# A decoder trunk on one core: decays from mid-chunk, corner products for four heads at once, and a joined first load

## The chip, the core and the metric

The kernel runs on one core of a Trainium2 chip. The metric is the device time of one execution in microseconds (us). The engines are named as the profile names them: PE is the matrix engine (PEld its weight loads), DVE the vector engine, ACT the scalar engine, POOL the GpSimd engine, SP the engine that issues most DMAs.

## The reference, cut to what matters

One decoder layer on 256 tokens, with 16 learned tokens put ahead (272 in all), width 2048, everything in float32:

```python
proj = rmsnorm(h) @ w_in
o_fox = forgetting_attention(fq, fk, fv, ff, b_forget)      # 8 heads of 128, causal softmax with decay
g_log = log_sigmoid(ga @ w_alpha2 + b_alpha) / 16
o_gla = gated_linear_attention(gq, gk, gv, g_log)           # 4 heads, keys 256, values 512 wide, chunks of 64
o_gla = head_rmsnorm(o_gla, gla_norm_g) * silu(gr)
y = sigmoid(gate_fox) * (o_fox @ w_o_fox) + sigmoid(gate_gla) * (o_gla @ w_o_gla)
h = h + y @ w_out
h = h + squared_relu(rmsnorm(h) @ w1) @ w2
out = rmsnorm(h)[:, 16:]
```

In the linear attention the logarithms of the decays are summed inside each chunk of 64 tokens (b). A query is multiplied by exp(b), a key by exp(-b), and a key that is seen from a later chunk also by the decays of the whole chunks between. The 272 tokens make four chunks of 64 and a fifth of 16.

## The kernel before

Activations lie with channels on the partitions and tokens along the free dimension. Every weight block of 128 output channels is streamed once from HBM in two halves (`raw`), cut into a high part by ACT (`whi`, line 120) and a remainder by DVE (`wlo`, line 121), both in the type fp32r; activations are cut into two parts likewise (`x`). A block is then either `gemm2` (lines 136 and 137: 512 columns with the high part, 256 with the remainder, for 16 slices) or, where all 272 tokens are wanted, `gemm_all` (lines 153 to 155: three products of 272 columns). Small products inside the attention (scores, transposes, parts of the outputs) are in plain float32, and such a product of line 518, 688, 739 or 740 stands as two records in the trace.

The order around the products is written by hand and then adjusted by a scheduler that simulates the program. `later(n, fn)` runs `fn` after n more blocks; so the attention's small products are put between the blocks of the streamed weights, in one queue of PE that is worked off in order. PSUM has three banks for blocks (`pg`) and five for everything else (`px`).

- Opening (lines 291 to 348): SP issues the first tile of `h`, two of seven weight blocks, the second tile of `h`, two more blocks, then three. `warm` is five products of ones that PE runs in the meantime (line 298). In stage 0 ACT makes `x` (line 311) and cuts the weights (line 266), DVE the remainders (lines 312 and 267).
- `decays(hd)` (line 386) makes, for a pair of key tiles of one GLA head, the running sums `za` (line 403), exp of them for queries (`eb_all`) and keys (`en_all`), and `ends`, the decay of each whole chunk (line 408).
- `gla_head(hd)` (line 468): `kx` holds per pair of chunks the keys, the keys carried into the next chunk and the next chunk's keys; `kd` the same carried one chunk further; `qd` the decayed queries, `rq` those of the later chunks carried back. `scores` (line 512) makes seven products, each over two key tiles: 48, 64, 64, 144, 64, 16 and 16 columns. The third to sixth have 128 columns of keys, the others 64. `turn` transposes the values; `vg` gathers the last 16 tokens of the head's four value tiles.
- `fox_head(hd)` (line 665): `scores`, `turn_v`, `turn_p` (lines 714 to 734) and `out_v` (line 736). The 272 tokens are 128 + 128 + 16 for keys and 16 + 128 + 128 for blocks of queries, so each head has two corners of 16 x 16 in its probabilities: transposes of 16 columns (lines 718, 729, 730), a product `vb` by `pT` with 144 columns and a product of the corner with 16 (line 740).

Of the kernel before, what the change touches and what calls it, by code (L numbers as in the profile page):

```python
# [7 lines left out]
F32 = mybir.dt.float32  # L8
# [57 lines left out]
def trunk(ctx: ExitStack, tc: tile.TileContext, hT, w_small, w_all, consts, w_alpha2, out):  # L66
# [222 lines left out]


    load_a, load_b = load_stage(0, 0), load_stage(0, 1)
    load_h(nc.sync, 0, 1)
    load_a(0, 2)
    load_h(nc.sync, 1, 1)
    load_a(2, 2)
    load_b(0, 3)
    for cols in (NT, NT, NT, NT, P):
        nc.tensor.matmul(warm[:, 0:cols], ones[:, 0:P], ones[:, 0:cols], start=True, stop=True)
    for s in range(1, 3):
        load_h(nc.sync, 2 * s, 2)  # L300
# [2 lines left out]
    for s in range(KT // 2):  # L303
# [5 lines left out]
        for kk in range(2):  # L309
            k = 2 * s + kk  # L310
            nc.scalar.activation(x[:, k, 0, :], h[:, k, 0:NA], AF.Identity, scale=gain(0, k))
# [68 lines left out]
    both = take(NA)  # L380
    fc = take(NA)[32:40]
    eb_all = lin.tile([P, 8, NT], F32, name="eb_all")
    ends = lin.tile([P, 8, 4], F32, name="ends")
    en_all = lin.tile([P, 8, NA], F32, name="en_all")

    def decays(hd):
# [21 lines left out]
        nc.vector.tensor_copy(ends[:, two, :], eb_all[:, two, C - NM - 1 : NT : C])  # L408
# [45 lines left out]
    NB = NA - 4 * C  # L454
    at0 = padded(lin, "at0", NT)
    at1 = padded(lin, "at1", NT - Q1)
    vz = padded(lin, "vz", P)
    az = padded(lin, "az", 4 * NB)
    v0 = [lin.tile([P, GLA_DV], F32R, name=n) for n in ("v0h", "v0l")]

# [7 lines left out]
    def gla_head(hd, sg, ready=None):  # L468
# [6 lines left out]
        qd = ready[0] if ready else att.tile([P, 2, NT], F32, tag="qd", name=nm("qd"))  # L475

        def keys(i, ps):
            def four(ap):
# [12 lines left out]
            for i in range(2):  # L491
                keys(i, gemm_all(next_weights(), x))
        for i in range(2):
            t = qd[:, i, :] if ready else total(gemm2(next_weights(), x[:, :, :, NM:NA]))
            nc.vector.scalar_tensor_tensor(qd[:, i, :], t, GLA_DK ** -0.5, eb[:, i, :], op0=ALU.mult, op1=ALU.mult)
        nc.vector.tensor_tensor(kx[:, :, :, C : 2 * C], kx[:, :, :, 0:C],
                                end[:, :, 0:4:2].unsqueeze(3).to_broadcast([P, 2, 2, C]), op=ALU.mult)

        kd = att.tile([P, 2, 2, 2 * C], F32, tag="kd", name=nm("kd"))
        nc.vector.tensor_tensor(kd, kx[:, :, :, C : 3 * C],  # L500
                                end[:, :, 1:4:2].unsqueeze(3).to_broadcast([P, 2, 2, 2 * C]), op=ALU.mult)

        rq = att.tile([P, 2, NT - Q1], F32, tag="rq", name=nm("rq"))
        nc.gpsimd.tensor_copy(rq[:, :, 0 : 2 * C], qd[:, :, Q1 : Q1 + 2 * C])
        nc.vector.tensor_tensor(rq[:, :, 2 * C :], qd[:, :, Q1 + 2 * C :], end[:, :, 3:4].to_broadcast([P, 2, NB]),
                                op=ALU.mult)
        nc.vector.tensor_tensor(rq[:, :, C:], rq[:, :, C:], end[:, :, 2:3].to_broadcast([P, 2, C + NB]), op=ALU.mult)

# [3 lines left out]
        def scores():  # L512
            pa = bank(px, "pa")
            p0, p1, pz = pa[:, 0:NT], pa[:, NT : 2 * NT - Q1], pa[0:C, 2 * NT - Q1 : 2 * NT - Q1 + NB]

            def score(dst, k, q):
                for a in range(2):
                    nc.tensor.matmul(dst, k[:, a], q[:, a, :], start=(a == 0), stop=(a == 1))  # L518

            Q0 = Q1 - C  # L520
# [19 lines left out]


        v1 = att.tile([P, GLA_DV], F32, tag="v1", name=nm("v1"))
        vg = att.tile([P, 4 * NB], F32, tag="vg", name=nm("vg"))
        pv = []

        def turn(i, vT):
# [3 lines left out]
            nc.tensor.transpose(pv[0][:, cols], vT[:, 0:P], ident)  # L550
            nc.tensor.transpose(pv[1][:, cols], vT[:, P : 2 * P], ident)
            if i == 3:
                p2 = bank(px, "p2")[0 : 4 * NB, 0:P]
# [3 lines left out]
                nc.scalar.copy(vz[0 : 4 * NB, :], p2)  # L557

        for i in range(4):
            ps = gemm_all(next_weights(), x)  # L560
# [57 lines left out]
    qd0 = att.tile([P, 2, NT], F32, tag="qd", name=nm("qd"))  # L618
    for i in range(2):
        total(first_ps[4 + i], qd0[:, i, :])  # L620
    ps = bank(pg, "psa")[:, 0:NA]
# [40 lines left out]
    vcs = [padded(late, f"vc{i}", P) for i in range(2)]  # L662
    pcs = [padded(late, f"pc{i}", NM) for i in range(2)]

    def fox_head(hd):
        fk = att.tile([P, NA], F32, tag="fk", name=nm("fk"))
# [41 lines left out]
        vc, pc = vcs[hd % 2], pcs[hd % 2]  # L708


        pT = att.tile([P, NM + P], F32, tag="pT", name=nm("pT"))
        nc.gpsimd.memset(pT[:, 0:NM], 0.0)

        def turn_v():
            pv = bank(px, "pv")
            nc.tensor.transpose(pv[:, 0:P], vT[:, 0:P], ident)
            nc.tensor.transpose(pv[:, P : 2 * P], vT[:, P : 2 * P], ident)
            nc.tensor.transpose(pv[0:NM, 2 * P : 3 * P], vT[:, 2 * P :], ident)
            va.extend(split(att, "va", pv[:, 0:P]))
            nc.scalar.copy(vb, pv[:, P : 2 * P])  # L720
            nc.scalar.copy(vc[0:NM, :], pv[0:NM, 2 * P : 3 * P])

        def turn_p():
            pt, pu = bank(px, "pt"), bank(px, "pu")
# [3 lines left out]
            nc.tensor.transpose(pt[:, 2 * P : 3 * P], pr_[:, q1 : q1 + P], ident)  # L728
            nc.tensor.transpose(pu[0:NM, 0:P], pr_[:, P : P + NM], ident)
            nc.tensor.transpose(pu[0:NM, P : 2 * P], pr_[:, q1 + 2 * P : q1 + NA], ident)  # L730
            nc.scalar.copy(pT[:, NM:], pt[:, 0:P])
            pa.extend(split(att, "pa", pt[:, P : 3 * P], 1))
            nc.vector.tensor_copy(pT[0:NM, 0:NM], pu[0:NM, P - NM : P])
            nc.vector.tensor_copy(pc[0:NM, :], pu[0:NM, 2 * P - NM : 2 * P])

        def out_v():
            po = bank(px, "pof")
            three(po[:, 0:NT], va, pa, True, False)
            nc.tensor.matmul(po[:, P - NM : NT], vb, pT, start=False, stop=False)
            nc.tensor.matmul(po[:, NT - NM : NT], vc, pc, start=False, stop=True)  # L740
# [256 lines left out]
```

## Time and profile before

| | before |
|---|---|
| median of 3 runs | 1609.93 us (1609.76 to 1610.15) |
| the profiled execution | 1609.59 us, its span 1607.9 us |
| granted clock of PE, mean | 0.998 |
| DVE busy | 1053.7 us (66%) |
| ACT busy | 787.4 us (49%) |
| POOL busy | 101.9 us (6%) |

The span runs from the first to the last instruction of the core; the execution's time is 1.7 us longer. A row of the timeline has the start in us from the beginning of the span, the us that the row covers, engine, line, operation, out<-in, the stationary and the moving operand, and xN, the number of records merged in it; what stands in brackets is the idle time before it and what ended it. PE records overlap, since their ends are modelled: what a product costs is read from the distance of its start to the start of the next. A group has the number of records, busy time, mean ns of one, and the idle time before them.

### The profile page before, as it was taken

Reading aid. Unit: us, or ns where it says so; the run is one execution under the profiler, and the core shown is the slowest. Engines: PE = TensorE matmul, PEld = TensorE weight load, DVE = VectorE, ACT = ScalarE, POOL = GpSimd, SP = SyncE. Lnnn points to the kernel's source line nnn. Section 1 sums busy time; section 2 is a strip of 40 time slices with the busy share of each in tenths; the row PEclk is TensorE's granted clock in tenths of the full one; section 3 lists DMA queues with packets and bytes.
Section 4 is the critical chain, followed back from the end, with each engine's and each line's share of the span. In section 5 each row is a group of like instructions: output and inputs, shape, how many; then the busy total and the mean of one; then the engine's idle time right before and its main releaser. Section 6 shows DMA issues by size and latency. Waiting matters only on the chain.

```text
span 1607.9 us, 25392 instructions
## 1 busy us (share of the span) xinstructions
PE 1597.0 (99%) x9878; PEld 1436.1 (89%) x9878; DVE 1053.7 (66%) x1603; ACT 787.4 (49%) x1221; POOL 101.9 (6%) x158
## 2 busy tenths in 40 slices
PE   9999999999999999999999999999999999999997
PEld 8999999999998888888888888888888888888887
DVE  7887757576655555555677776567655776567655
ACT  7655444454445444444555544444444444444563
POOL 1011000110000000000011000000000000000022
PEclk9999999999999999999999999999999999999999
DMA  9454545554555566556566555665565555656552
GB/s 322 156 160 146 182 154 177 184 171 158 158 158 180 187 187 190 187 187 190 174 203 188 186 190 188 188 189 187 187 193 186 189 188 189 191 186 190 185 183 97
DMA packets 86745, 293.09 MB, mean 182 GB/s; under 512 B 9128, under 2 KB 17072, under 8 KB 86496
## 3 DMA queue, kind: packets, MB, share of 16 engines
q1 hardware_dynamic: 86016, 289.62, 56.9%
q8 instruction: 77, 1.26, 0.3%
q0 software_dynamic: 176, 1.12, 0.2%
q10 hardware_dynamic: 432, 0.72, 0.1%
q14 instruction: 44, 0.36, 0.1%
HBM read 289.32 MB, written 2.11 MB: 181 GB/s over the span
## 4 chain that ended last, share of the span: by engine, by line
PE 99%; DMA 0%; issue 0%; POOL 0%; SPq 0%; ACT 0%; POOLq 0%; DVE 0%; ACTq 0%
PE ps L136 51%; PE ps L137 26%; PE psa L155 5%; PE psa L154 5%; PE psa L153 5%; PE ps L328 1%; PE pa L518 1%; PE ps L866 1%; PE ps L333 1%; PE ps L850 0%; DMA raw<-w_all_dram 0%; PE po L584 0%; POOL o L914 0%; PE pq L688 0%; PE p L550 0%
## 5 line engine op out<-in xcount | busy, mean ns | idle before, releaser
L121 DVE TENSOR_TENSOR wlo<-raw,whi 128x1024 fp32r<-128x1024 f32 x522 | 640.8, 1228 | 462.6 <-ACT whi L120 461.8
L120 ACT CAST whi<-raw 128x1024 fp32r<-128x1024 f32 x522 | 548.0, 1050 | 732.6 <-PE ps L136 502.9
L136 PE MATMUL ps<-x,whi 128*128 128x512 f32 x1952 | 685.9, 394 | 0.0
L137 PE MATMUL ps<-x,wlo 128*128 128x256 f32 x1952 | 547.8, 281 | 0.0
L136 PEld LDWEIGHTS ps<-x,whi 128*128 128x128 f32 x1952 | 366.4, 188 | 83.2
L137 PEld LDWEIGHTS ps<-x,wlo 128*128 128x128 f32 x1952 | 367.4, 188 | 0.2
L136 PE MATMUL ps<-a,whi 128*128 128x512 f32 x960 | 335.8, 395 | 0.0
L137 PE MATMUL ps<-a,wlo 128*128 128x256 f32 x960 | 269.9, 282 | 0.0
L136 PEld LDWEIGHTS ps<-a,whi 128*128 128x128 f32 x960 | 180.1, 188 | 40.8
L137 PEld LDWEIGHTS ps<-a,wlo 128*128 128x128 f32 x960 | 181.7, 189 | 0.3
L155 PE MATMUL psa<-x,whi 128*128 128x272 f32 x624 | 181.3, 291 | 0.0
L153 PE MATMUL psa<-x,whi 128*128 128x272 f32 x624 | 181.3, 290 | 0.0
L154 PE MATMUL psa<-x,wlo 128*128 128x272 f32 x624 | 179.7, 288 | 0.0
L153 PEld LDWEIGHTS psa<-x,whi 128*128 128x128 f32 x624 | 118.2, 189 | 0.5
L154 PEld LDWEIGHTS psa<-x,wlo 128*128 128x128 f32 x624 | 117.5, 188 | 0.0
L155 PEld LDWEIGHTS psa<-x,whi 128*128 128x128 f32 x624 | 117.2, 188 | 0.1
L136 PE MATMUL ps<-og,whi 128*128 128x512 f32 x256 | 89.9, 393 | 0.0
L136 PE MATMUL ps<-y,whi 128*128 128x512 f32 x256 | 89.1, 392 | 0.0
L792 POOL TENSOR_TENSOR acc<-acc,hsq 128x256 f32<-128x256 f32 x26 | 28.4, 1092 | 771.4 <-ACT hsq L791 771.4
L137 PE MATMUL ps<-y,wlo 128*128 128x256 f32 x256 | 71.8, 281 | 0.0
L137 PE MATMUL ps<-og,wlo 128*128 128x256 f32 x256 | 71.8, 280 | 0.0
L165 DVE TENSOR_TENSOR evt<-ps,evb 128x256 f32<-128x256 f32 x158 | 65.8, 417 | 0.2 <-ACT evb L162 0.2
(294 smaller groups left out, 1413.4 us busy)
## 6 DMA issues: line engine op xcount, KB each, us to landing
raw<-w_all_dram SPq DMA_DIRECT2D x537, 512.0 KB, 3.9
raw<-w_all_dram SPq DMA_DIRECT2D x8, 384.0 KB, 6.6
h<-hT_dram SPq DMA_DIRECT2D x7, 275.0 KB, 7.0
negc<-fdram POOLq DMA_DIRECT2D x1, 1088.0 KB, 6.3
out_dram<-o SPq DMA_DIRECT2D x2, 512.0 KB, 2.7
raw<-w_all_dram SPq DMA_DIRECT2D x2, 256.0 KB, 3.6
out_dram<-o ACTq DMA_DIRECT2D x2, 256.0 KB, 3.0
room<-w_small_dram SPq DMA_DIRECT2D x1, 320.0 KB, 7.7
```

The source lines that it names most:

```text
L120: nc.scalar.copy(hi[:, k, :], r)
L121: nc.vector.tensor_tensor(lo[:, k, :], r, hi[:, k, :].bitcast(F32), op=ALU.subtract)
L136: nc.tensor.matmul(ps, hi, x, start=first, stop=False)
L137: nc.tensor.matmul(ps[:, 0:NT], lo, x[:, 0, :], start=False, stop=last)
L153: nc.tensor.matmul(ps[:, 0:n], hi, x[:, k, 0, :], start=(k == 0), stop=False)
L154: nc.tensor.matmul(ps[:, 0:n], lo, x[:, k, 0, :], start=False, stop=False)
L155: nc.tensor.matmul(ps[:, 0:n], hi, x[:, k, 1, :], start=False, stop=(k == KT - 1))
L165: nc.vector.tensor_tensor(t, ps[:, 0:NT], b, op=ALU.add)
L328: nc.tensor.matmul(ps, hi, x[:, k, :, NM:NA], start=st, stop=False)
L333: nc.tensor.matmul(ps[:, 0:NT], lo, x[:, k, 0, NM:NA], start=False, stop=sp)
L518: nc.tensor.matmul(dst, k[:, a], q[:, a, :], start=(a == 0), stop=(a == 1))
L792: nc.gpsimd.tensor_tensor(acc, acc, sq, op=ALU.add)
```

## The change

1. In `decays` the running sums are counted from the middle of each chunk: half of a chunk's last sum is taken off all its sums before the exponentials. `ends` then holds five factors for carrying a query or key across chunks, made by a small exponential.
2. In GLA's scores the queries lie in one tile `qx` with the carried copies beside the own ones. Two products, of 208 and 80 columns, replace the four with 128 columns of keys (64, 144, 64 and 16). `kd` and `rq` are gone; keys are carried once. The product of the last 16 tokens moves ahead of the two.
3. In FoX the corners of four heads are gathered by POOL (`vg`, `pgr`), transposed together and multiplied in one product, masked by `same`, and added to the output after every fourth head (`out_corners`, `fill_corners`). The per-head corner transposes and the corner product go, and `pT` has 128 columns instead of 144.
4. In the opening `h`'s first two tiles are one load, `warm` has four products, and the first two weight blocks are cut slice by slice.
5. In GLA the padded tile of the last 16 tokens is the transpose's input (`vg`, 128 columns) instead of its output.

```diff
-    load_h(nc.sync, 0, 1)
+    load_h(nc.sync, 0, 2)
     load_a(0, 2)
-    load_h(nc.sync, 1, 1)
     load_a(2, 2)
     load_b(0, 3)
-    for cols in (NT, NT, NT, NT, P):
+    for cols in (NT, NT, NT, NT):
         nc.tensor.matmul(warm[:, 0:cols], ones[:, 0:P], ones[:, 0:cols], start=True, stop=True)
...
             if s == 0:
-                wa[3](2 * kk, 2)
+                wa[3](0, 2, slice(kk, kk + 1))
...
         if s == 0:
+            wa[3](2, 2)
...
+        e, half = ends[:, two, :], tmp.tile([P, 2, 4], F32, tag="half", name=nm("half"))
+        nc.vector.tensor_scalar(half, za[:, :, C - 1 : 4 * C : C], 0.5, None, op0=ALU.mult)
+        nc.vector.tensor_tensor(e[:, :, 1:4], half[:, :, 0:3], half[:, :, 1:4], op=ALU.add)
+        nc.vector.tensor_tensor(e[:, :, 4:5], e[:, :, 2:3], e[:, :, 3:4], op=ALU.add)
+        nc.vector.tensor_copy(e[:, :, 0:1], half[:, :, 3:4])
+        nc.scalar.activation(e, e, AF.Exp, scale=1.0 / 16.0)
+        four = za[:, :, 0 : 4 * C].rearrange("p a (c s) -> p a c s", s=C)
+        nc.vector.tensor_tensor(four, four, half.unsqueeze(3).to_broadcast([P, 2, 4, C]), op=ALU.subtract)
...
-        nc.vector.tensor_copy(ends[:, two, :], eb_all[:, two, C - NM - 1 : NT : C])
...
-            nc.vector.scalar_tensor_tensor(qd[:, i, :], t, GLA_DK ** -0.5, eb[:, i, :], op0=ALU.mult, op1=ALU.mult)
+            for q, n, at in ((0, Q1, 0), (Q1, Q3, NT)):
+                nc.vector.scalar_tensor_tensor(qx[:, i, at : at + n], t[:, q : q + n], GLA_DK ** -0.5,
+                                               eb[:, i, q : q + n], op0=ALU.mult, op1=ALU.mult)
...
-        nc.vector.tensor_tensor(kd, kx[:, :, :, C : 3 * C],
-                                end[:, :, 1:4:2].unsqueeze(3).to_broadcast([P, 2, 2, 2 * C]), op=ALU.mult)
...
-        nc.gpsimd.tensor_copy(rq[:, :, 0 : 2 * C], qd[:, :, Q1 : Q1 + 2 * C])
...
+        def seen(dst, src, c):
+            nc.vector.tensor_tensor(dst, src, end[:, :, c : c + 1].to_broadcast(list(dst.shape)), op=ALU.mult)
...
+        q2, q3, qz = (qx[:, :, NT + c : NT + d] for c, d in ((0, C), (C, Q3), (Q3, Q3 + NB)))
+        nc.gpsimd.tensor_copy(qz, q3[:, :, C:])
+        seen(q3[:, :, C:], q3[:, :, C:], 0)
+        seen(qx[:, :, Q1 : Q1 + C], q2, 2)
+        seen(qx[:, :, Q1 + C : NT], q3, 4)
...
-            score(p0[0:C, 0:Q0], kx[:, :, 0, 0:C], qd[:, :, 0:Q0])
-            score(p1[0:C, 0:C], kx[:, :, 1, 0:C], qd[:, :, Q1 : Q1 + C])
-            score(p0[:, Q0:Q1], kx[:, :, 0, C:], qd[:, :, Q0:Q1])
-            score(p0[:, Q1:], kd[:, :, 0, :], rq)
-            score(p1[:, C : 2 * C], kx[:, :, 1, C:], qd[:, :, Q1 + C : Q1 + 2 * C])
-            score(p1[:, 2 * C :], kd[:, :, 1, :], qd[:, :, Q1 + 2 * C :])
-            score(pz, kz.rearrange("p a b t -> p a (b t)"), qd[:, :, Q1 + 2 * C :])
+            score(p0[0:C, 0:Q0], kx[:, :, 0, 0:C], qx[:, :, 0:Q0])
+            score(p1[0:C, 0:C], kx[:, :, 1, 0:C], q2)
+            score(pz, kz.rearrange("p a b t -> p a (b t)"), qz)
+            score(p0[:, Q0:], kx[:, :, 0, C:], qx[:, :, Q0:NT])
+            score(p1[:, C:], kx[:, :, 1, C:], q3)
...
+    def corners(t):
+        return t.rearrange("p (c q) -> p c q", q=P)[:, :, P - NM :]
...
+        for c in range(2):
+            nc.gpsimd.tensor_copy(vg[:, four, c, :], vT[:, P * (1 + c) : P * (1 + c) + NM])
...
-            nc.tensor.transpose(pv[0:NM, 2 * P : 3 * P], vT[:, 2 * P :], ident)
...
-            nc.scalar.copy(vc[0:NM, :], pv[0:NM, 2 * P : 3 * P])
...
+            for c, at0 in ((0, P), (1, q1 + 2 * P)):
+                nc.gpsimd.tensor_copy(pgr[:, four, c, :], pr_[:, at0 : at0 + NM])
...
-            nc.tensor.transpose(pu[0:NM, 0:P], pr_[:, P : P + NM], ident)
-            nc.tensor.transpose(pu[0:NM, P : 2 * P], pr_[:, q1 + 2 * P : q1 + NA], ident)
...
-            nc.tensor.matmul(po[:, P - NM : NT], vb, pT, start=False, stop=False)
-            nc.tensor.matmul(po[:, NT - NM : NT], vc, pc, start=False, stop=True)
+            nc.tensor.matmul(po[:, P:NT], vb, pT, start=False, stop=True)
...
+            nc.scalar.copy(og4[:, four], corners(po[:, 0:NT]))
+
+        def out_corners():
+            pu = bank(px, "pu")
+            vz, pz = (t.rearrange("p h c t -> p (h c t)") for t in (vg, pgr))
+            nc.tensor.transpose(pu[:, 0:P], vz, ident)
+            nc.tensor.transpose(pu[:, P : 2 * P], pz, ident)
+            nc.scalar.copy(vz, pu[:, 0:P])
+            nc.vector.tensor_tensor(pz.rearrange("p (b q) -> p b q", q=NM), same,
+                                    pu[:, 2 * P - NM : 2 * P].unsqueeze(1).to_broadcast([P, NC, NM]), op=ALU.mult)
+            later(1, lambda: fill_corners(pu, vz, pz))
+
+        def fill_corners(pu, vz, pz):
+            nc.tensor.matmul(pu[:, 2 * P : 3 * P], vz, pz, start=True, stop=True)
+            nc.vector.tensor_tensor(og4, og4, pu[:, 2 * P : 3 * P].rearrange("p (h c q) -> p h c q", c=2, q=NM),
+                                    op=ALU.add)
+            hi, lo = (of[:, hd - 3 : hd + 1, o, :].rearrange("p h (c q) -> p h c q", q=P)[:, :, :, P - NM :]
+                      for o in range(2))
+            split_to(hi, lo, og4)
...
+        if four == 3:
+            later(3, out_corners)
```

As the changed program is laid out on PE, `out_corners`' transposes follow the `vb` product of head 3, and stand between `out_v`'s first and second product for head 7. The corner product follows one block later. After head 7 the first eight k-slices of the output projection's two FoX blocks run four and four: the part that reads heads 0 to 3 comes ahead of 19 products of the next block, the part that reads heads 4 to 7 behind them. In GLA's first head the first score products stand 28 products into the fourth value block (3 before).

More of the change, by code (lines that the diff above doesn't have):

```diff
@@ L382, in trunk @@
     eb_all = lin.tile([P, 8, NT], F32, name="eb_all")
-    ends = lin.tile([P, 8, 4], F32, name="ends")
+    ends = lin.tile([P, 8, 5], F32, name="ends")
     en_all = lin.tile([P, 8, NA], F32, name="en_all")
@@ L456, in trunk @@
     at1 = padded(lin, "at1", NT - Q1)
-    vz = padded(lin, "vz", P)
+    vg = padded(lin, "vg", P)
     az = padded(lin, "az", 4 * NB)
@@ L474, in gla_head @@
         kz = att.tile([P, 2, 4, NB], F32, tag="kz", name=nm("kz"))
-        qd = ready[0] if ready else att.tile([P, 2, NT], F32, tag="qd", name=nm("qd"))
+        qx = att.tile([P, 2, 2 * NT - 6 * NB], F32, tag="qx", name=nm("qx"))
+        Q0, Q3 = Q1 - C, NT - Q1
         def keys(i, ps):
@@ L493, in gla_head @@
         for i in range(2):
-            t = qd[:, i, :] if ready else total(gemm2(next_weights(), x[:, :, :, NM:NA]))
-            nc.vector.scalar_tensor_tensor(qd[:, i, :], t, GLA_DK ** -0.5, eb[:, i, :], op0=ALU.mult, op1=ALU.mult)
-        nc.vector.tensor_tensor(kx[:, :, :, C : 2 * C], kx[:, :, :, 0:C],
-                                end[:, :, 0:4:2].unsqueeze(3).to_broadcast([P, 2, 2, C]), op=ALU.mult)
-        kd = att.tile([P, 2, 2, 2 * C], F32, tag="kd", name=nm("kd"))
-        nc.vector.tensor_tensor(kd, kx[:, :, :, C : 3 * C],
-                                end[:, :, 1:4:2].unsqueeze(3).to_broadcast([P, 2, 2, 2 * C]), op=ALU.mult)
-        rq = att.tile([P, 2, NT - Q1], F32, tag="rq", name=nm("rq"))
-        nc.gpsimd.tensor_copy(rq[:, :, 0 : 2 * C], qd[:, :, Q1 : Q1 + 2 * C])
-        nc.vector.tensor_tensor(rq[:, :, 2 * C :], qd[:, :, Q1 + 2 * C :], end[:, :, 3:4].to_broadcast([P, 2, NB]),
-                                op=ALU.mult)
-        nc.vector.tensor_tensor(rq[:, :, C:], rq[:, :, C:], end[:, :, 2:3].to_broadcast([P, 2, C + NB]), op=ALU.mult)
+            t = ready[0][:, i, :] if ready else total(gemm2(next_weights(), x[:, :, :, NM:NA]))
+            for q, n, at in ((0, Q1, 0), (Q1, Q3, NT)):
[3 more added lines that the diff above has]
+            nc.vector.tensor_tensor(dst, src, end[:, :, c : c + 1].to_broadcast(list(dst.shape)), op=ALU.mult)
+        nc.vector.tensor_tensor(kx[:, :, :, C : 2 * C], kx[:, :, :, 0:C],
+                                end[:, :, 1:4:2].unsqueeze(3).to_broadcast([P, 2, 2, C]), op=ALU.mult)
+        q2, q3, qz = (qx[:, :, NT + c : NT + d] for c, d in ((0, C), (C, Q3), (Q3, Q3 + NB)))
[3 more added lines that the diff above has]
+        seen(qx[:, :, Q1 + C : NT], q3, 4)
         def scores():
@@ L542, in gla_head @@
         v1 = att.tile([P, GLA_DV], F32, tag="v1", name=nm("v1"))
-        vg = att.tile([P, 4 * NB], F32, tag="vg", name=nm("vg"))
+        vz = att.tile([P, P], F32, tag="vz", name=nm("vz"))
         pv = []
@@ L552, in turn @@
             if i == 3:
-                p2 = bank(px, "p2")[0 : 4 * NB, 0:P]
+                p2 = bank(px, "p2")[:, 0:P]
                 nc.tensor.transpose(p2, vg, ident)
@@ L556, in turn @@
                 nc.scalar.copy(v1, pv[1])
-                nc.scalar.copy(vz[0 : 4 * NB, :], p2)
+                nc.scalar.copy(vz, p2)
         for i in range(4):
@@ L617, in trunk @@
     ts = [total(ps) for ps in first_ps[0:4]]
-    qd0 = att.tile([P, 2, NT], F32, tag="qd", name=nm("qd"))
+    qd0 = att.tile([P, 4, NT], F32, tag="so", name=nm("qd"))[:, 0:2, :]
     for i in range(2):
@@ L661, in trunk @@
     BL = ((0, NM + P, 0), (1, NA, NM + P))
-    vcs = [padded(late, f"vc{i}", P) for i in range(2)]
-    pcs = [padded(late, f"pc{i}", NM) for i in range(2)]
+    NC = P // NM
+    same = scan[:, 0:P].rearrange("p (b q) -> p b q", q=NM)
+    nc.gpsimd.memset(same, 1.0)
+    for sign, base in ((-1, 0), (1, NM - 1)):
+        nc.gpsimd.affine_select(same, same, pattern=[[sign * NM, NC], [0, NM]], compare_op=ALU.is_ge, fill=0.0,
+                                base=base, channel_multiplier=-sign)
+    corner = {}
+    def corners(t):
+        return t.rearrange("p (c q) -> p c q", q=P)[:, :, P - NM :]
     def fox_head(hd):
@@ L707, in fox_head @@
         vb = att.tile([P, P], F32, tag="vb", name=nm("vb"))
-        vc, pc = vcs[hd % 2], pcs[hd % 2]
-        pT = att.tile([P, NM + P], F32, tag="pT", name=nm("pT"))
-        nc.gpsimd.memset(pT[:, 0:NM], 0.0)
+        pT = att.tile([P, P], F32, tag="pT", name=nm("pT"))
+        four = hd % 4
+        if four == 0:
+            corner["v"], corner["p"], corner["o"] = (att.tile([P, 4, 2, NM], F32, tag=t, name=nm(t), bufs=1)
+                                                     for t in ("vg", "pgr", "og4"))
+        vg, pgr, og4 = corner["v"], corner["p"], corner["o"]
+        for c in range(2):
+            nc.gpsimd.tensor_copy(vg[:, four, c, :], vT[:, P * (1 + c) : P * (1 + c) + NM])
         def turn_v():
@@ L728, in turn_p @@
             nc.tensor.transpose(pt[:, 2 * P : 3 * P], pr_[:, q1 : q1 + P], ident)
[L729 to L731 removed]
+            nc.scalar.copy(pT, pt[:, 0:P])
             pa.extend(split(att, "pa", pt[:, P : 3 * P], 1))
[L733 to L734 removed]
         def out_v():
```

3 lines of the change are left out of this document (1 added, 2 removed).

## The prediction

> **What bounds the kernel now.** I read the page first, then PE's waits, then the timeline of PE around the small products and of the first 12 us.
>
> ```profile
> span 1607.9 us, 25392 instructions
> PE 1597.0 (99%) x9878; PEld 1436.1 (89%) x9878; DVE 1053.7 (66%) x1603; ACT 787.4 (49%) x1221; POOL 101.9 (6%) x158
> ```
>
> PE is busy for 1597.0 of 1607.9 us. As ends of products are modelled, that alone proves nothing; what does is the view of PE's waits, which holds three waits in all, each one time:
>
> ```profile
> PE warm L298 <- DVE ones L189: 1.3, 1, 1.3
> PE ps L328 <- ACT whi L266: 1.0, 1, 1.0
> PE pn L890 <- ACT sq L871: 0.7, 1, 0.7
> ```
>
> Two lie in the opening, one in the tail. In between PE never stops for weights, a bank or an operand. So each record that leaves PE's queue there takes its whole spacing off the time, work moved to DVE, ACT and POOL costs nothing unless it makes PE stop, and outside that stretch only the opening is changed.
>
> **GLA's scores.** First the scores of the last head, then the end of a FoX output; start, us covered, engine, line, operands, records. The first row merges eight records of 64 key columns and the four of the second row, which a window that begins later shows alone.
>
> ```profile
> 283.72 1.27 PE L518 MATMUL pa<-qd,kx 128*64 128x48 f32 x12
> 284.33 0.66 PE L518 MATMUL pa<-qd,kx 128*128 128x64 f32 x4
> 284.82 0.71 PE L518 MATMUL pa<-rq,kd 128*128 128x144 f32 x4
> 285.37 0.56 PE L518 MATMUL pa<-qd,kx 128*128 128x64 f32 x4
> 285.76 0.57 PE L518 MATMUL pa<-qd,kd 128*128 128x16 f32 x4
> 286.26 0.40 PE L518 MATMUL pa<-qd,kz 128*64 128x16 f32 x4
> 286.60 0.33 PE L550 MATMUL p<-cons,vT 128*128 128x128 f32 x1
> ...
> 395.74 0.41 PE L739 MATMUL pof<-pT,vb 128*128 128x144 f32 x2
> 395.99 0.29 PE L740 MATMUL pof<-pc,vc 128*128 128x16 f32 x2
> 396.13 0.49 PE L688 MATMUL pq<-fk,fq 128*128 128x144 f32 x2
> 396.36 0.38 PE L153 MATMUL psa<-x,whi 128*128 128x272 f32 x1
> ```
>
> Starts give what each product takes. The four with 128 key columns run from 284.33 to 286.26: 1.93 us for 16 records, though their columns differ from 16 to 144. Those with 64 and 16 columns need 0.89 us for eight (285.37 to 286.26), 0.1125 each, however short; two of 144 need 0.25 (395.74 to 395.99), 0.125 each. So there is a floor, and above it I take time by the column: 208 columns cost 0.125 x 208 / 144 = 0.18, an estimate from this row, since no row has that width; 80 columns lie on the floor. After the change four records of 208 (0.72) and four of 80 (0.45) stand for 12 x 0.1125 + 4 x 0.125 = 1.85: 0.68 saved. Besides, the product with 64 key columns that now stands at the end (286.26 to 286.60, 0.34 for four, where eight took 0.61 at the front) joins its like, which spares a change of width and back, about 0.1. I take 0.80 a head, nearer to the sum of both, 3.2 us for four; bounds 0.68 and 0.90, 2.7 to 3.6 us. The wider transpose of the last 16 tokens keeps its 128 moving columns: nothing.
>
> **FoX's corners.** Two products of a value block, and the turn of the probabilities:
>
> ```profile
> 402.60 0.29 PE L154 MATMUL psa<-x,wlo 128*128 128x272 f32 x1
> 402.72 0.29 PE L155 MATMUL psa<-x,whi 128*128 128x272 f32 x1
> ...
> 408.98 0.27 PE L728 MATMUL pt<-cons,pr 128*128 128x128 f32 x1
> 409.09 0.27 PE L729 MATMUL pu<-cons,pr 128*16 128x128 f32 x1
> 409.20 0.27 PE L730 MATMUL pu<-cons,pr 128*16 128x128 f32 x1
> ```
>
> A transpose out of 16 columns takes the same 0.11 us as one out of 128. Three a head go: 0.33. The corner's two records of 16 columns take 0.14 by the starts at 395.99 and 396.13, but what follows a short record starts early; by the GLA rows they are worth 2 x 0.1125 = 0.22. The 144 columns that become 128 give 2 x 0.01. Together 0.57 a head (0.49 at the lower end), 4.6 us for eight (3.9). Each four heads add two transposes and two records of 128 columns: 2 x 0.11 + 2 x 0.1125 = 0.45, so 0.9. Net 3.6 us, from 4.6 - 0.9 and 0.1 for the places where PE changes from blocks to the new products; bounds 2.8 and 3.8.
>
> What the new steps wait for: the transposes in `out_corners` wait for POOL's copies.
>
> ```profile
> L563 POOL COPY vg<-vT 128x16 f32<-128x16 f32 x16 | 8.4, 526 | 102.7 <-DVE vT L562 102.7
> ```
>
> Such a copy takes 0.53 us. The last two of a group can start when head 3's probabilities are scaled, before its turn of probabilities; a value block of 48 products lies between that and the transposes, at 0.125 us each (0.12 between 402.60 and 402.72, rounded) 6.0 us. That hides 1.1 us. Without it PE would lose those 1.1 us twice. On POOL the next group's first copy waits until the corner product has read the old tile; behind it stand the next head's masks, needed a head later. At the end of FoX the added chain (product, sum, two cuts) is covered by the 35 products that run before slices four to seven are read.
>
> **The added work on DVE, and GLA's first head.** The halves, three sums and a copy are tiny; the subtraction covers 512 elements, four query products stand for two, and `kd`'s 512 elements shrink to 128.
>
> ```profile
> 77.64 0.17 DVE L408 COPY ends<-eb_all 128x8 f32<-128x8 f32 x1
> 81.52 0.41 DVE L481 TENSOR_TENSOR kx<-ps,en_all 128x256 f32<-128x256 f32 x1
> 81.98 0.41 DVE L481 TENSOR_TENSOR kx<-psa,en_all 128x256 f32<-128x256 f32 x1
> 82.21 0.32 PE L518 MATMUL pa<-qd,kx 128*64 128x48 f32 x2
> 82.91 0.56 PE L518 MATMUL pa<-qd,kx 128*64 128x48 f32 x6
> L500 DVE TENSOR_TENSOR kd<-kx,ends 128x512 f32<-128x512 f32 x4 | 2.7, 685 | 0.0
> ```
>
> At 0.17 for a tiny one and 0.69 for 512 elements the chain from running sums to `kx` gets about 4 x 0.17 + 0.69 + 0.3 (more query products), with the small exponential between: some 1.5 to 2 us, and a weight cut may fall inside. In heads 1 to 3 the decays are ready a block or more ahead. In head 0 PE's scores now stand 0.28 us behind the end of `kx` (81.93 to 82.21) and 0.5 at the second group. They move back by 25 products of 0.125, 3.1 us. That covers the longer chain, narrowly. I charge 0.2 us, bounds 0 and 1.0: if the cover fails, the value block behind waits too, as PE's queue is in order.
>
> **The opening.** Rates in two windows (columns end with the clock, DMA share, GB/s), then the timeline:
>
> ```profile
> 3.00:5.00 2.00, 2.00 (x6) 1.56 (x6) 0.65 (x2) 1.14 (x2) 0.33 (x2) 1.00 0.82 205
> 5.00:8.00 3.00, 1.97 (x11) 1.37 (x10) 1.74 (x3) 1.58 (x4) 0.00 (x0) 1.00 0.99 325
> ...
> 1.72 0.46 SPq L273 DMA_DIRECT2D h<-hT_dram  x1
> 2.22 0.94 SPq L261 DMA_DIRECT2D raw<-w_all_dram  x2
> ...
> 3.01 0.52 ACT L311 ACTIVATE x<-h 128x272 fp32r<-128x272 f32 x1 [0.92 <-DMA h<-hT_dram]
> 4.20 0.62 ACT L266 CAST whi<-raw 128x512 fp32r<-128x512 f32 x1 [0.67 <-DMA raw<-w_all_dram]
> 6.46 0.62 ACT L266 CAST whi<-raw 128x512 fp32r<-128x512 f32 x1 [0.34 <-DMA raw<-w_all_dram]
> 9.95 1.96 ACT L266 CAST whi<-raw 128x1024 fp32r<-128x1024 f32 x2 [0.55 <-DMA raw<-w_all_dram]
> ...
> 1.27 4.03 PE L298 MATMUL warm<-ones 128*128 128x256 f32 x10 [1.27 <-DVE ones L189]
> 5.06 0.71 PE L328 MATMUL ps<-x,whi 128*128 128x512 f32 x2
> 7.13 1.19 PE L328 MATMUL ps<-x,whi 128*128 128x512 f32 x4 [1.03 <-ACT whi L266]
> 11.46 1.56 PE L328 MATMUL ps<-x,whi 128*128 128x512 f32 x6
> ```
>
> PE starts at 5.06, stops at about 6.1 and runs without a gap from 7.13, released by the third load of the queue. With `h` joined, SP issues the weights behind it 0.5 us earlier (the row at 1.72), in a stretch where DMA moves 205 GB/s and later 325: there is room. The first weight load waits for a second tile of `h` (128 x 275 floats, 0.14 MB), some 0.4 us at 325 GB/s; but both slices of two blocks can then run, and fill the old gap. Cutting one slice first saves half of a 0.62 us cut. So PE starts near 5.1 as before, and the next two blocks are cut at about 6.5. Stage 0 took 4.3 us from 7.13 and some 0.9 before it; 5.2 us of work without a gap end near 10.3. Stage 1's cut starts on its load at 9.95 and ends about 11.0, half a us before use at 11.46; that load too comes about 0.5 earlier, so stage 1 begins near 10.6. Gain 0.8 us, bounds -0.3 (the longer first load delays all and the DMA gives nothing back) and 1.2. The missing `warm` product costs nothing in itself, since PE waits there.
>
> **Sum.** 3.2 + 3.6 + 0.8 - 0.2 = 7.4 us off the profiled execution's 1609.59: 1602.2. The median of the runs shown, 1609.93, lies 0.3 higher: **1602.5**. The ends of the terms give 8.6 and 4.2 off: 1601.3 and 1605.7.
>
> **Rivals.** (1) The opening gives nothing or 0.3 back: 1603.3 to 1603.6. For it: at 8 us and later the loads run one behind another, and stage 1 stands on its load. Against: the slack at 205 GB/s. Chance 0.18.
>
> (2) PE's clock rises later. The ten `warm` records have 2304 columns in the 3.79 us until 5.06, 1.64 ns a column, against 0.87 at 395.74: PE ran at half rate there, and one product less ends that stretch 0.4 us sooner. If the rise then takes another such stretch, half of 3.8 us is lost: 1.9 us, 1604.4. Against: PE stood idle for a us before 7.13 and kept its rate (six of 512 columns in 1.56 us at 11.46). Chance 0.06. The Trainium skill ("TensorE: Matmul & The Clock Gate", Part 1, What's actually happening) has a free-running window of about 3.4 us that must be busy before the clock doubles; by that figure at most 1.7 us would be lost, an estimate, and the trace agrees with the halving.
>
> (3) The change doesn't do what it says to PE: time goes by columns, of which the scores have 416 before and after. At 0.87 ns a column the wide scores cost 1.0 both ways, the corner product 0.03 and the shorter `vb` 0.03; left are the transposes, 8 x 0.39 - 0.9 = 2.2, and 0.6 of the other terms: 1607.1. Against: 16 and 64 columns both take 0.11. Chance 0.05. The Trainium skill (same page, Back-to-back issue gap) states N/2.4 + 2.5 ns for an isolated product and a floor of about 25 ns; by these figures GLA would gain some 0.05 us a head and the corner product 0.05, and the sum would be about 3.1 off, an estimate. The row of 16 columns, 0.1125, speaks against it here.
>
> (4) Slower: a bank. `pu` is now held from the fourth head's output until the corner product one block later, among five banks. If the next head's turn must wait for it, PE stops for a block, 48 x 0.125 = 6.0 us, twice: 1602.5 + 12.0 = 1614.5. It ends slower by over 0.2% (about 3.2 us, what a measurement of this kernel can tell from no change) once the two holds exceed 5.3 us each. For it: PE has a single queue. Against: a head took five banks and takes four now, and no wait for a bank shows. Chance 0.05.
>
> **How the numbers follow.** Forecast 0.66, rivals 0.18, 0.06, 0.05, 0.05. Range 1601.2 to 1605.2: the forecast's upper bounds, rivals 1 and 2, and most of the forecast's lower end; (3), (4) and some tails stay out. Forecast, (1) and (2) are faster by over 0.2%: 0.90; (3) is within 0.2%: 0.05; (4) slower: 0.05.
>
> **What would show it.** In the changed profile: eight wide score records in about 1.2 us, those of 208 columns 0.18 apart; three waits of PE, none in the attention; the first unbroken product before 6 us and stage 1 near 10.6; one corner product per four heads. Wrong if 208 columns cost much over 0.18, if PE's waits name POOL or DVE at `pu` or GLA's first scores, or if stage 1 still starts at 11.4.

## The result and the profile after

The changed kernel takes 1602.26 us (median, 1601.62 to 1602.67), the kernel before in the same comparison 1609.84 (1609.76 to 1610.15): ratio 0.9952, 95% interval 0.994 to 0.9965, 7.6 us less. The profiled execution of the changed kernel took 1601.62 us. First two lines of its page, then all the waits of PE (times: total, count, longest, us):

```profile
span 1599.9 us, 25296 instructions
PE 1590.0 (99%) x9812; PEld 1428.7 (89%) x9812; DVE 1055.5 (66%) x1618; ACT 787.5 (49%) x1230; POOL 109.7 (7%) x181
```

```profile
PE warm L297 <- DVE ones L189: 1.3, 1, 1.3
PE pn L932 <- ACT sq L913: 0.7, 1, 0.7
```

PE has 66 records less and is still the bound. The wait on `whi` in the opening is gone from this view, and none has appeared in the attention. Next the timeline of the changed kernel: the scores of the last GLA head (the third row merges the products of 208 and 80 columns), then the end of the third FoX head's output.

```profile
279.86 0.29 PE L155 MATMUL psa<-x,whi 128*128 128x272 f32 x1
280.08 0.68 PE L531 MATMUL pa<-qx,kx 128*64 128x48 f32 x8
280.59 0.36 PE L531 MATMUL pa<-qx,kz 128*64 128x16 f32 x4
280.88 1.38 PE L531 MATMUL pa<-qx,kx 128*128 128x208 f32 x8
282.09 0.27 PE L560 MATMUL p<-cons,vT 128*128 128x128 f32 x1
...
389.75 0.38 PE L761 MATMUL pof<-pT,vb 128*128 128x128 f32 x2
389.97 0.41 PE L709 MATMUL pq<-fk,fq 128*128 128x144 f32 x2
390.12 0.38 PE L153 MATMUL psa<-x,whi 128*128 128x272 f32 x1
```

The eight wide records take 1.21 us (280.88 to 282.09) where sixteen took 1.93. From the start of `vb` to the next block's start FoX needs 0.37 us (389.75 to 390.12), where it needed 0.62 (395.74 to 396.36).

Where the difference lies is read best from three starts of PE that every kernel has: its first record of line 199 (the end of the opening), the last transpose of GLA's values (line 550, 560 in the changed kernel), and its last record of line 199, behind the attention and the outputs. In the changed kernel:

```profile
45.35 0.29 PE L199 MATMUL prb<-csh,ones 128*128 128x272 f32 x1
...
294.15 0.27 PE L560 MATMUL p<-cons,vT 128*128 128x128 f32 x1
...
882.68 0.28 PE L199 MATMUL pn<-csh,ones 128*128 128x256 f32 x1
```

The same three rows in every trace give this table (us; from the third start to the last stretch of the tail it is 707.5 in all). The kernels below the first two are the experiments.

| kernel | opening | GLA stretch | FoX stretch | median time |
|---|---|---|---|---|
| before | 46.15 | 252.56 | 592.01 | 1609.84 |
| changed | 45.35 | 248.79 | 588.53 | 1602.26 |
| opening alone | 46.28 | 252.56 | 592.01 | 1609.45 |
| GLA alone | 46.46 | 248.79 | 592.06 | 1606.41 |
| FoX alone | 46.58 | 252.56 | 588.39 | 1606.19 |
| 208 split | 45.93 | 249.69 | 588.53 | 1603.17 |
| 128 keys everywhere | 45.44 | 249.85 | 588.53 | 1603.14 (one run) |
| last product last | 45.83 | 250.06 | 588.53 | 1603.43 (one run) |
| bank held longer | 46.50 | 248.79 | 588.54 | 1603.12 (one run) |
| one `warm` product | 46.51 | 248.79 | 588.53 | 1603.49 |
| more slices | 45.32 | 248.79 | 588.53 | 1601.77 |
| changed, again | 45.14 | 248.79 | 588.53 | 1601.67 |

Between the two profiled executions the opening gave 0.80, GLA 3.77 and FoX 3.48, 8.0 in all. The two stretches behind the opening repeat to about 0.01 us from run to run of the same code; the opening doesn't. The medians come from four comparisons, in which the kernel before took between 1609.84 and 1610.46, so those of different rows are less comparable than the stretches.

### The profile page after: what moved, and what is told of

Same layout as the page of the kernel before. It is cut to its first block, busy times and chain, and to the rows that moved or that the text cites. A ratio compares the mean times of both kernels' runs of the same rounds, so it can differ in the third digit from the quotient of the medians.

```text
span 1599.9 us, 25296 instructions
## 1 busy us (share of the span) xinstructions
PE 1590.0 (99%) x9812; PEld 1428.7 (89%) x9812; DVE 1055.5 (66%) x1618; ACT 787.5 (49%) x1230; POOL 109.7 (7%) x181
## 3 DMA queue, kind: packets, MB, share of 16 engines
q8 instruction: 77, 1.26, 0.3%
## 4 chain that ended last, share of the span: by engine, by line
PE 99%; DMA 0%; issue 0%; POOL 0%; ACT 0%; DVE 0%; SPq 0%; POOLq 0%; ACTq 0%
PE ps L136 51%; PE ps L137 26%; PE psa L155 5%; PE psa L154 5%; PE psa L153 5%; PE ps L328 1%; PE ps L333 1%; PE ps L908 1%; PE pa L531 1%; PE ps L892 0%; DMA raw<-w_all_dram 0%; PE po L594 0%; POOL o L956 0%; PE po L182 0%; PE psa L637 0%
```

## The experiments

**One part at a time.** The kernel before with part 4 alone.

> The kernel before with part 4 alone (the joined load of h, four warm products, the first weight cuts by slices). Theory (the terms of the three changed places add up, each is paid where its records stand): PE's first row of line 199 starts near 45.35 instead of 46.15, and the whole run is 0.8 us shorter than before, near 1609.0. Rival (the opening's gain is given back later, and GLA and FoX hold the whole difference): the same start at line 199 as before and no change in the time.

```diff
-    load_h(nc.sync, 0, 1)
+    load_h(nc.sync, 0, 2)
     load_a(0, 2)
-    load_h(nc.sync, 1, 1)
...
-    for cols in (NT, NT, NT, NT, P):
+    for cols in (NT, NT, NT, NT):
...
-                wa[3](2 * kk, 2)
+                wa[3](0, 2, slice(kk, kk + 1))
...
+            wa[3](2, 2)
```

1609.45 against 1610.04 for the kernel before on that chip: 0.6 less, ratio 0.9995 with an interval of 0.9986 to 1.0005, so the time alone doesn't settle it. Its profiled execution reached line 199 at 46.28, not at 45.35, later even than the first profile of before. Everything behind line 199 takes exactly what it took before, which refutes "given back later": what the opening gives is given in the opening, but it is not 0.8 each time. What delayed it is taken up below.

The kernel before with parts 1, 2 and 5 alone (their diff stands above).

> The kernel before with parts 1, 2 and 5 alone (decays from mid-chunk, two wide score products, the last 16 tokens padded at the transpose's input). In the two traces at hand the four heads stand 3.8 us shorter, 0.94 a head. Theory A (a floor for each record, and a change between narrow and wide stationary operands that costs about 0.2 us each time): 3.8 us shorter than before, near 1606.0. Theory B (the prediction's own term, with about 0.1 for the change of width): 3.2 us shorter, near 1606.6. Theory C (time by columns, 416 both before and after): no change.

1606.41, 3.6 less than before (ratio 0.9976, 0.9967 to 0.9986). The GLA stretch is 248.79, to the digit that of the changed kernel: 3.77 less, 0.94 a head. The median lies between theories A and B; the stretch, which repeats to 0.01, decides for 3.8. That number had been read from the changed kernel's trace, so this run shows that the gain is GLA's alone, not where it comes from. C is out.

The kernel before with part 3 alone.

> The kernel before with part 3 alone (the corners of four heads in one product). The prediction's term gives 3.6 us less, the two traces at hand 3.5: near 1606.2. By columns alone (transposes 2.2, small terms 0.5) it would be 2.7 less, near 1607.1. If the bank of the corner product held PE up, its waits would name line 773 or the next head's turn, and the time would be longer than before.

1606.19, 3.85 less (ratio 0.9978, 0.9968 to 0.9988); its FoX stretch is 3.62 shorter. The prediction's term holds, columns alone do not, and PE's waits name no bank. Together with GLA the same part gave 3.48: the difference, 0.14, builds up in shifts of less than 0.02 from one product to the next along the streamed blocks, where no wait is named. GLA alone has 0.05 more in that stretch than the kernel before, though its FoX code is the same. The cause stays open.

**What a score record costs.** The changed kernel with one product split.

> The changed kernel with the score product of 208 columns split again into one of 64 and one of 144, the same columns and the same keys. Floor theory: per head four records of 0.1125 and four of 0.125 stand for four of 0.18, 0.23 more a head, 0.9 more in all than the changed kernel: near 1603.2, some 6.7 less than before. Column theory: no change against the changed kernel, near 1602.3, some 7.6 less than before.

```diff
-            score(p0[:, Q0:], kx[:, :, 0, C:], qx[:, :, Q0:NT])
+            score(p0[:, Q0:Q1], kx[:, :, 0, C:], qx[:, :, Q0:Q1])
+            score(p0[:, Q1:], kx[:, :, 0, C:], qx[:, :, Q1:NT])
```

```profile
282.12 1.61 PE L531 MATMUL pa<-qx,kx 128*128 128x64 f32 x12
283.56 0.27 PE L561 MATMUL p<-cons,vT 128*128 128x128 f32 x1
```

In this kernel's timeline twelve wide records of the last head take 1.44 us (282.12 to 283.56) where eight of the same columns took 1.21: 0.23 a head, as the floor theory said. The stretch grows by 0.89; the median, 1603.17, is 0.91 above the changed kernel's of the first comparison. The number of columns did not change; the number of records did, so it is records that cost.

The changed kernel with 128 columns of keys in the three narrow products too.

> The changed kernel with 128 columns of keys in the three narrow score products of a head too (the rows more are not read), so that no product of the scores changes width. Theory: 12 records a head go from 0.058 to 0.112, +0.65, and the change to narrow and back, some 0.3 by the run that moved the last narrow product, is spared: +0.35 a head, 1.4 in the stretch between line 199's first row and the last transpose of GLA's values, so about 250.2 there. If a change of width costs as much as it saves in records or more: no more than 248.8.

```diff
-            score(p0[0:C, 0:Q0], kx[:, :, 0, 0:C], qx[:, :, 0:Q0])
-            score(p1[0:C, 0:C], kx[:, :, 1, 0:C], q2)
+            score(p0[:, 0:Q0], kx[:, :, 0, 0 : 2 * C], qx[:, :, 0:Q0])
+            score(p1[:, 0:C], kx[:, :, 1, 0 : 2 * C], q2)
...
-        kz = att.tile([P, 2, 4, NB], F32, tag="kz", name=nm("kz"))
+        kz = att.tile([P, 2, 8, NB], F32, tag="kz", name=nm("kz"))
```

```profile
280.77 1.00 PE L531 MATMUL pa<-qx,kx 128*128 128x48 f32 x8
281.61 0.57 PE L531 MATMUL pa<-qx,kz 128*128 128x16 f32 x4
282.03 1.35 PE L531 MATMUL pa<-qx,kx 128*128 128x208 f32 x8
```

The moving columns are the same as in the changed kernel, 48, 64 and 16, and only the stationary operand is wider. Twelve records now take 1.26 us (280.77 to 282.03) where they took 0.80 (280.08 to 280.88): 0.105 a record against 0.067, edges included; inside a group the starts lie 0.112 and 0.058 apart. So the floor is set by the columns of the stationary operand (they are also the rows of the result; the runs don't part the two). That the stretch grew by 1.05 and not by 1.4 is head 0's doing: there the narrow and the wide products stand between different blocks, and nothing was lost; heads 1 to 3 lost 0.36 each, as expected. With 12 x 0.054 = 0.65 for the records, 0.29 is what a change to 64 columns and back costs. The Trainium skill ("TensorE: Matmul & The Clock Gate", LDWEIGHTS (loading the stationary operand)) gives a load as its columns divided by 1.2, in ns: 107 for 128 and 53 for 64. The 0.112 and 0.058 agree with that within about 5 ns.

The changed kernel with the narrow product of the last 16 tokens behind the wide ones again.

> The changed kernel with the product of the last 16 tokens behind the two wide ones again, same records. If a change between 64 and 128 columns of keys costs PE about 0.2 us, it is paid once more in each head, and what follows has 128: up to 0.25 a head, 1.0 in all, in the stretch between line 199's first row and the last transpose of GLA's values. If the order costs nothing, that stretch stays at 248.79.

```diff
-            score(pz, kz.rearrange("p a b t -> p a (b t)"), qz)
             score(p0[:, Q0:], kx[:, :, 0, C:], qx[:, :, Q0:NT])
             score(p1[:, C:], kx[:, :, 1, C:], q3)
+            score(pz, kz.rearrange("p a b t -> p a (b t)"), qz)
```

```profile
281.50 1.98 PE L531 MATMUL pa<-qx,kx 128*64 128x48 f32 x16
283.42 0.41 PE L531 MATMUL pa<-qx,kz 128*64 128x16 f32 x4
283.75 0.33 PE L560 MATMUL p<-cons,vT 128*128 128x128 f32 x1
```

The same 20 records, and the stretch is 1.27 longer, 0.32 a head, somewhat more than expected. Scores to first transpose take 2.25 us (281.50 to 283.75) instead of 2.01 (280.08 to 282.09); the rest falls on the transposes behind. The order alone is thus worth a third of GLA's gain.

What a change of width costs is seen in the loads of the stationary operands, PEld's rows, first of the changed kernel, then of the one with 128 keys everywhere:

```profile
279.74 0.19 PEld L155 LDWEIGHTS psa<-x,whi 128*128 128x128 f32 x1
280.07 0.54 PEld L531 LDWEIGHTS pa<-qx,kx 128*64 128x64 f32 x8 [0.15 <-issue]
280.54 0.31 PEld L531 LDWEIGHTS pa<-qx,kz 128*64 128x64 f32 x4
280.88 1.23 PEld L531 LDWEIGHTS pa<-qx,kx 128*128 128x128 f32 x8
```

```profile
280.52 0.19 PEld L155 LDWEIGHTS psa<-x,whi 128*128 128x128 f32 x1
280.65 0.99 PEld L531 LDWEIGHTS pa<-qx,kx 128*128 128x128 f32 x8
281.55 0.53 PEld L531 LDWEIGHTS pa<-qx,kz 128*128 128x128 f32 x4
```

Eight loads of 64 columns take 0.47 us (280.07 to 280.54) and eight of 128 take 0.90 (280.65 to 281.55): the loads follow each other as closely as the products do. At a change of width the next load comes late. The first narrow one starts 0.33 behind the block's last load, where the same load with 128 columns starts 0.13 behind it; the last four narrow ones fill 0.34 until the first wide one, where four take 0.23 otherwise. That is 0.31 in all, near the 0.29 and 0.32 above. Why a load of another width starts late no run shows.

**The bank.** The changed kernel with FoX's corner product one block later.

> The changed kernel with the corner product of FoX one block later, so that its bank is held for two blocks instead of one. Prediction's view (there are banks to spare): the stretch between the last transpose of GLA's values and line 199's last row stays at 588.5. Bank rival: a turn or an output behind it must wait for the bank, PE's waits name it, and the stretch grows by up to 6 us for each of the two holds.

```diff
-            later(1, lambda: fill_corners(pu, vz, pz))
+            later(2, lambda: fill_corners(pu, vz, pz))
```

From the waits of all engines, first of the changed kernel, then of this one:

```profile
POOL vg L738 <- PE pu L778: 4.8, 1, 4.8
```

```profile
POOL vg L738 <- PE pu L778: 10.6, 1, 10.6
```

The FoX stretch stays (588.54). POOL's first copy of the next group waits 5.8 us longer for the corner product and nobody notices; PE's waits name no bank, even at twice the hold. The bank rival is refuted. This kernel's single time is 0.9 us above the changed kernel's median; its opening, 46.50, ends 1.15 later than in the changed kernel's profile.

**The opening.** The changed kernel with one `warm` product.

> The changed kernel with one warm product instead of four. Clock theory (the rise of PE's clock counts from when PE is first kept busy): PE has half rate until about 4 us after its first real product, up to 1.9 us more, near 1604.2. If the warm products only fill a wait, no difference beyond 0.3.

```diff
-    for cols in (NT, NT, NT, NT):
+    for cols in (NT,):
```

```profile
4.90 1.22 PE L328 MATMUL ps<-x,whi 128*128 128x512 f32 x2 [2.41 <-ACT whi L266]
...
6.35 1.91 PE L328 MATMUL ps<-x,whi 128*128 128x512 f32 x4
...
9.72 0.62 PE L328 MATMUL ps<-x,whi 128*128 128x512 f32 x2
```

Two records of 512 columns take 1.22 us at 4.90 and 0.62 at 9.72. In this kernel's timeline PE, idle for 2.41 us beforehand, runs at half that rate at first; the trace's first record of the full clock begins at 9.12 us. (The clock column of the window view counts the time before that record as 1.00, here and in the rows of the prediction, so the half rate is seen in the distance of the records alone.) It costs 1.8: a median of 1603.49 (1602.84 to 1604.71) against 1601.67 (1601.59 to 1602.62) for the changed kernel on the same chip; between the two profiles the opening differs by 1.4. The clock theory holds: `warm` is no filler. The Trainium skill ("TensorE: Matmul & The Clock Gate", Part 1, What's actually happening) says the clock doubles after a free-running window of about 3.4 us in which PE was kept busy; a rise 4.2 us after PE's restart at 4.90 fits that.

More cuts by slices, and the changed kernel itself on the same chip.

> The changed kernel with two more cuts by slices: the second pair of weight blocks in stage 0 and the first cut of stage 1. If PE's start of stage 1 hangs on the cuts, its stop at 6.5 (0.3) and its stop ahead of stage 1 (0.25) shrink: 0.3 to 0.5 less than the changed kernel, near 1601.8. If it hangs on when the loads land, the time moves by no more than its own spread of some 0.5, with no shift of the median.

```diff
+                if s == 1:
+                    for ks in range(2):
+                        wa[3](0, 4, slice(ks, ks + 1))
+                else:
+                    wa[3](0, 4)
...
-            wa[3](2, 2)
+            for kk in range(2):
+                wa[3](2, 2, slice(kk, kk + 1))
```

> The changed kernel itself, on the same chip as the other opening runs. If all that differs from one execution to the next lies in the opening, the stretch from PE's first row of line 199 to its last product is again 1544.85 us to the last digit, and the execution's time follows that first row; near 1602.3.

1601.77 with more slices (1601.37 to 1601.97), 1601.67 without (1601.59 to 1602.62). No shift of the median, so slices give nothing that can be measured here, and no version came out that beats the changed kernel. The changed kernel repeated its 1544.85 us from line 199 to the tail exactly, and its opening came out at 45.14 instead of 45.35.

What the openings differ in is seen in the timelines of the changed kernel and of the opening alone, whose SP issues its first loads at the same times:

```profile
0.81 0.39 SPq L273 DMA_DIRECT2D h<-hT_dram  x1
3.64 0.93 ACT L310 ACTIVATE x<-h 128x272 fp32r<-128x272 f32 x2 [1.55 <-DMA h<-hT_dram]
...
9.48 1.87 ACT L266 CAST whi<-raw 128x1024 fp32r<-128x1024 f32 x2 [0.38 <-DMA raw<-w_all_dram]
10.58 1.65 PE L328 MATMUL ps<-x,whi 128*128 128x512 f32 x6
```

```profile
0.81 0.39 SPq L273 DMA_DIRECT2D h<-hT_dram  x1
4.05 0.93 ACT L310 ACTIVATE x<-h 128x272 fp32r<-128x272 f32 x2 [1.96 <-DMA h<-hT_dram]
...
10.37 1.96 ACT L266 CAST whi<-raw 128x1024 fp32r<-128x1024 f32 x2 [0.40 <-DMA raw<-w_all_dram]
11.47 1.68 PE L328 MATMUL ps<-x,whi 128*128 128x512 f32 x6 [0.28 <-ACT whi L266]
```

The first `h` lands at 3.64 in the one and 4.05 in the other, stage 1's weights at 9.48 and 10.37, and stage 1 starts 1.1 us behind that in both. The same issues land up to 0.9 us apart in these two. Over all seven profiles with this opening the last load of stage 0 releases its cut between 6.71 us (128 keys everywhere) and 8.56 (bank held longer), and stage 1 starts between 10.37 and 11.73. In each of the seven stage 1 starts 1.1 us behind its first cut, which a load releases, and line 199 follows 34.8 us later: the landing of stage 1's weights sets where the opening ends. The moment at which PE's rate doubles moves as well: its first two records of 512 columns took 0.74 us in the changed kernel's profile,

```profile
4.92 0.74 PE L328 MATMUL ps<-x,whi 128*128 128x512 f32 x2
```

and 1.22 in that of the kernel with 208 split, whose opening code is the same:

```profile
5.05 1.22 PE L328 MATMUL ps<-x,whi 128*128 128x512 f32 x2
```

## Why the prediction was right, point by point

The bound, the stretch in which it holds and the rule "each record that leaves PE's queue takes its spacing off" were right: the rows in which records are dropped or split follow from counting them, while the order of records, which the prediction had at 0.1 a head, counted for more. The forecast for the profiled execution was 7.4 less; 8.0 came, and the medians moved by 7.6.

- **GLA's scores**, 0.80 a head: 0.94 came, 3.77 for four, above the bound of 3.6. In the last head 0.72 lies between the wide groups (1.93 less 1.21), where the prediction had 0.68; 208 columns cost 0.176 each, forecast 0.18. Another 0.15 lies in the narrow records (0.61 and 0.34 less 0.80), where it had 0.1 for the change of width. And 0.06 lies behind the scores, which it left out: from the first transpose to the third product of the next block pass 0.53 us (286.60 to 287.13) in the kernel before and 0.47 (282.09 to 282.56) in the changed one. That is 0.93 of the 0.94.

```profile
287.13 0.29 PE L155 MATMUL psa<-x,whi 128*128 128x272 f32 x1
```

```profile
282.56 0.28 PE L155 MATMUL psa<-x,whi 128*128 128x272 f32 x1
```

The mis-sized term is the change of width. By the order alone it is worth 0.32 a head, and a part of it stands in what the prediction counted as records. The run with the last product last parts them: 2.50 for the records (252.56 less 250.06, 0.63 a head) and 1.27 for the order make the 3.77.
- **The rule of the Trainium skill on short products** ("TensorE: Matmul & The Clock Gate", Back-to-back issue gap), by which the prediction let GLA gain 0.05 a head (its formula gives 0.08, an estimate), is not the one that counts for these products: it is for an isolated product, and the run with 128 keys everywhere shows the width of the stationary operand in its place.
- **FoX's corners**, 3.6: 3.62 alone and 3.48 together. In the run with FoX alone the value transpose gave 0.11 a head, the two of the probabilities 0.21 and the corner 0.24, 4.5 for eight against 4.6 forecast. Two transposes (0.22) and one corner product (0.21) per four heads cost 0.43, forecast 0.45:

```profile
409.37 0.27 PE L770 MATMUL pu<-cons,vg 128*128 128x128 f32 x1
409.48 0.27 PE L771 MATMUL pu<-cons,pgr 128*128 128x128 f32 x1
409.59 0.41 PE L709 MATMUL pq<-fk,fq 128*128 128x144 f32 x2
...
416.24 0.38 PE L778 MATMUL pu<-pgr,vg 128*128 128x128 f32 x2
416.45 0.27 PE L742 MATMUL pv<-cons,vT 128*128 128x128 f32 x1
```

POOL's copies cost nothing, as forecast. Their groups in the changed kernel give 0.22 and 0.20 us each, where the row that the prediction used had 0.53:

```profile
L751 POOL COPY pgr<-pr 128x16 f32<-128x16 f32 x16 | 3.5, 224 | 34.1 <-DVE pr L721 34.0
L738 POOL COPY vg<-vT 128x16 f32<-128x16 f32 x16 | 2.6, 196 | 79.8 <-DVE vT L726 75.0 <-PE pu L778 4.8
```

- **The stall in GLA's first head**, 0.2: none. The first score stands at 84.52 instead of 82.21; with the opening's 0.80 that is 3.1 us further back, as forecast, and no wait appeared. Head 0 gave 0.95, like the others.
- **The opening**, 0.8: 0.80 in the first pair of profiles, which was luck in part. Over the seven profiles with the new opening line 199 starts at 45.78 on average (45.14 to 46.50), over the three with the old one at 46.40 (46.15 to 46.58): 0.6. Stage 1 came at 10.58 in the changed kernel's profile, as forecast, and the old stop of 1.0 us is gone there; a stop of 0.2 remains at 6.5. But in the profiles of the same opening stage 1 starts anywhere from 10.37 to 11.73, twice later than the 11.4 that the prediction named as a sign of being wrong. With the old opening stage 1 stood 4.3 us of unbroken work behind the stop (7.13 to 11.46); with the new one it stands 1.1 us behind the landing of its weights, which differs by 1.4 us (9.26 to 10.63). So the stop no longer counts, as the prediction had it, but the landing does, and for that it named no spread: its bounds were hardly wider than what one execution differs from the next.
- **The rivals.** Opening without gain: the profiles give some 0.6 on average, and the time of the opening alone can't tell that from zero, so this rival isn't refuted. Clock: shown as a mechanism by the run with one `warm` product, 1.8 us of the 1.9 worked out, but leaving out one of five did not bring it about: the full rate begins between 4.6 and 7.1 us with four and between 4.6 and 6.5 with five. Columns: refuted by the split and by GLA alone. Bank: refuted with the hold doubled.

By the median of the first comparison several errors met: GLA gave 0.6 more than forecast and the stall of 0.2 didn't come, while FoX and the opening gave less (3.5 for 3.6; 0.3 for 0.8, which is 7.58 less the 7.23 of all that lies behind the opening). That the sum came out to 0.2 us is luck in part. A forecast as close as that does not show that each term was.

## What to carry to other kernels

When PE is the bound, count records and the columns of their stationary operands before moving columns: with a stationary operand of 128 columns a float32 record cost the same here from 16 to 128 moving columns (0.112 us; 144 cost 0.122 and 208 cost 0.176), so products that share an operand's width should be merged and placed next to each other. Put products of one width together; here the order of the same 20 records was worth 0.3 us a head. Compare two kernels stretch by stretch between instructions that both have: what repeats to 0.01 us can be settled by one profile, and what doesn't needs several before a fraction of a us is believed.

## What the runs showed of the hardware

Small float32 products with a stationary operand of 128 columns follow each other every 0.112 us and with 64 columns every 0.058, whether 16 or 64 columns move, and the loads of these operands do the same; going to 64 and back to 128 costs 0.29 to 0.32 us beyond that. The same loads, issued at the same time, landed up to 1.8 us apart within the first 11 us, by the cuts that they release. By the traces' first record of the full clock PE's rate doubled between 4.6 and 7.1 us in the eleven profiles whose `warm` products keep PE busy from 1.3 us on, with the same opening code too, and at 9.1 us where PE had been idle for 2.4 us before its first product.
